# Query, key, gmlp-input and gate projections of a decoder layer as Strassen pairs kept in DRAM, with both attentions after them

## The chip, the cores and the metric

The kernel runs on one core of one Trainium2 chip. The metric is the device time of one execution in microseconds (us). A core has a matrix engine (TensorE, PE in the profile; its weight loads are the row PEld), a vector engine (VectorE, DVE), an activation engine (ScalarE, ACT), a general engine (GpSimd, POOL) and a queue from which the DMAs of this kernel are issued (SyncE, SP). On-chip tiles lie in SBUF, matmul results in eight PSUM banks, inputs, outputs and spilled tiles in DRAM.

## The reference

One layer (DEPTH is 1) for 1024 prompt positions and 64 sample positions (8 sequences of 8), model width 1024, all in float32:

```python
h = rmsnorm(x, norm_mix)
q, k, v, gu, gv, ga, gb = split_in(h @ w_in)      # 1024, 256, 256, 768, 768, 1024, 1024 columns
o = sink_attention(q, k, v, ...)                  # 16 heads of 64, 4 key heads, window 128, blocks of 128
vn = layernorm(gelu(gv), ln_g, ln_b)
s = gelu(gu) * (lower_triangular(ws) @ vn + bs)   # inside chunks of 128 positions, 6 groups of 128
merged = sigmoid(ga) * (o @ w_pa) + sigmoid(gb) * (s @ w_pb)
x = x + merged @ w_out
x = x + conv_ffn(rmsnorm(x, norm_ffn))            # up, causal conv of width 3, gelu gate, down
```

A final RMSNorm follows. Keys, values, convolution rows and normalised gmlp rows are outputs too.

## The kernel before

**Number format.** Every float32 operand of a matmul is split into a rounded high part and a remainder (`split`, L39 to L41: a ScalarE copy, then a VectorE subtraction), and a product is three matmuls: high by high, high weight by low operand, low weight by high operand. `mm3` (L215) does this for one tile of 128 output columns: 8 steps over the inner dimension, 3 matmuls each, over the token chunks of a group.

**Tokens.** They form two groups. Group 0 has 576 columns (64 sample, 512 prompt), in chunks of 320 and 256. Group 1 has 512 columns in one chunk.

**Weights.** The class `Weights` holds a list of weight tiles in the order of their use. It loads them by DMA into four raw buffers (`wraw`), splits them some units ahead (`emit`, tiles `wh`, `wl`), and `W.get()` hands out the next. In this order each weight of the first half stands twice, once per group.

**First half, per group** (the loop `for gr in groups`, L408 on): eight query tiles, two key tiles, the values (token-major, L551: activations are the stationary operand, 256 weight columns move), sixteen gate tiles, attention, gmlp inputs (`gu_tile`, and token-major gv), layer norm, the chunk mixing (`mix`, L863), then per output tile the two branch products with their gates (L901 to L907), then the output projection (`x1_tile`). Group 1 repeats this.

**Attention** (L709 on) runs in 16 steps per group, four key heads by four blocks. A step has three parts: `sc_p` (8 score matmuls, L727, then the softmax on ScalarE, VectorE and GpSimd), `tr_p` (4 transposes, L752, a split into `ph` and `pl`, and four GpSimd selections, L763), and `pv_p` (4 matmuls of 512 columns, L775, then a copy and additions, L777 and L782, and a split into `qo`). Parts of three steps overlap:

```python
for i in range(len(steps) + 2):
    if i >= 2:
        tr_p(*steps[i - 2])
    fill()
    if i < len(steps):
        sc_p(*steps[i])
    fill()
    if i >= 2:
        pv_p(*steps[i - 2])
```

`fill()` issues independent matmul work between the parts. Before, this is the gates: 32 half tiles of 4 inner steps (`gate_pieces`, L576), written to DRAM and read back for the merge. Group 0 has a sample attention of six iterations ahead of its steps (`sc_s`, L645, reads cached keys `ckt`).

**Second half.** The feed-forward block uses Strassen's scheme (7 products of half matrices in place of 8) for pairs of weight tiles: the class `Chain` (L1081) does the 7 products of one pair for one token group, 12 matmuls each (L1107) of 288 or 256 columns, in three PSUM banks. Its operands are 7 sums of activation halves per group, split (`tx`), and 7 sums of weight quarters (`total`, L165). The down projection (L1252) uses the scheme as well.

A scheduler in the build orders the instructions of each engine. On each engine, and on the SP queue, they then run in that order.

## Time and profile before

| what | value |
|---|---|
| median of 3 runs | 1609.77 us (1608.27 to 1610.48) |
| profiled execution | 1607.9 us, span 1605.9 us |
| PE / DVE / ACT / POOL busy in the span | 98% / 70% / 49% / 20% |
| DMA of the kernel | 215.07 MB, 40.1% of 16 DMA engines |
| first half, second half | 0 to 877 us, 877 to 1605.9 us |

"Busy" of an engine is the union of its instructions' durations. A matmul's duration holds its way through the array, so matmuls overlap, and the rate is read from how many start in a stretch. In the chain of waits a piece such as "PE mm L222 x762" is a run of matmuls that wait for nothing but each other.

### The profile page before, as it was taken

Reading aid. Unit: us, or ns where it says so; the run is one execution under the profiler, and the core shown is the slowest. Engines: PE = TensorE matmul, PEld = TensorE weight load, DVE = VectorE, ACT = ScalarE, POOL = GpSimd, SP = SyncE. Lnnn points to the kernel's source line nnn. Section 1 sums busy time; section 2 is a strip of 40 time slices with the busy share of each in tenths; the row PEclk is TensorE's granted clock in tenths of the full one; section 3 lists DMA queues with packets and bytes.
Section 4 is the critical chain, followed back from the end, with each engine's and each line's share of the span. In section 5 each row is a group of like instructions: output and inputs, shape, how many; then the busy total and the mean of one; then the engine's idle time right before and its main releaser. Section 6 shows DMA issues by size and latency. Waiting matters only on the chain.

```text
span 1605.9 us, 28256 instructions
## 1 busy us (share of the span) xinstructions
PE 1575.6 (98%) x11148; PEld 1490.7 (93%) x11148; DVE 1122.3 (70%) x1659; ACT 789.3 (49%) x1536; POOL 316.6 (20%) x432
## 2 busy tenths in 40 slices
PE   8999999999999999999999899999999999999997
PEld 8989999999998888898878899999999999999996
DVE  8546873654548777646457878898889778785676
ACT  7434664333345365544334555565565446353452
POOL 1302330100040343301002222222223222000023
PEclk9999999999999999999999999999999999999998
DMA  6322224134553622242565233332233225983453
GB/s 205 129 100 90 86 87 155 39 106 141 181 188 131 213 99 91 95 140 82 157 213 192 96 101 114 116 137 91 92 117 128 102 83 190 334 269 94 122 165 129
DMA packets 84147, 216.86 MB, mean 135 GB/s; under 512 B 9648, under 2 KB 15856, under 8 KB 84016
## 3 DMA queue, kind: packets, MB, share of 16 engines
q1 hardware_dynamic: 83872, 215.07, 40.1%
q8 instruction: 87, 1.43, 0.4%
q14 instruction: 44, 0.36, 0.1%
q10 hardware_dynamic: 144, 0.01, 0.0%
HBM read 168.82 MB, written 48.19 MB: 135 GB/s over the span
## 4 chain that ended last, share of the span: by engine, by line
PE 83%; DVE 7%; ACT 3%; POOL 2%; DMA 2%; issue 2%; SPq 0%; DVEq 0%; POOLq 0%; ACTq 0%
PE mm L222 32%; PE st L1107 28%; PE dn L1252 11%; PE mm L551 6%; DVE wl L41 2%; ACT s L742 1%; DMA wraw<-wt 1%; PE sc L727 1%; PE po L775 1%; POOL pl L763 1%; PE mm L863 1%; PE pt L752 1%; POOL ph L763 1%; DVE tl L41 1%; DVE nm L739 0%
## 5 line engine op out<-in xcount | busy, mean ns | idle before, releaser
L222 PE MATMUL mm<-hm,wh 128*128 128x320 f32 (+2 forms) x1920 | 429.7, 332 | 5.4 <-ACT hm L44 5.1
L1107 PE MATMUL st<-th,wl 128*128 128x288 f32 (+1 forms) x1232 | 356.3, 290 | 4.0 <-DVE wl L41 4.0
L1107 PE MATMUL st<-th,wh 128*128 128x288 f32 (+1 forms) x1232 | 357.6, 290 | 1.7 <-ACT wh L40 1.7
L1107 PE MATMUL st<-tl,wh 128*128 128x288 f32 (+1 forms) x1232 | 357.1, 290 | 0.0
L222 PEld LDWEIGHTS mm<-hm,wh 128*128 128x128 f32 x1920 | 302.0, 189 | 34.3 <-ACT hm L44 5.1
L40 ACT CAST wh<-wraw 128x512 fp32r<-128x512 f32 (+2 forms) x235 | 186.4, 801 | 236.7 <-PE mm L222 113.7
L222 PE MATMUL mm<-hm,wl 128*128 128x320 f32 (+1 forms) x960 | 264.4, 329 | 0.0
L41 DVE TENSOR_TENSOR wl<-wraw,wh 128x512 fp32r<-128x512 f32 (+2 forms) x235 | 220.5, 948 | 37.5 <-ACT wh L40 34.8
L1107 PEld LDWEIGHTS st<-th,wl 128*128 128x128 f32 x1232 | 234.4, 190 | 4.6 <-DVE wl L41 4.6
L1107 PEld LDWEIGHTS st<-th,wh 128*128 128x128 f32 x1232 | 234.9, 191 | 2.9 <-ACT wh L40 2.3
L1107 PEld LDWEIGHTS st<-tl,wh 128*128 128x128 f32 x1232 | 234.7, 191 | 0.0
L1252 PE MATMUL dn<-th,wh 128*128 128x288 f32 (+1 forms) x616 | 177.9, 289 | 2.5 <-DVE x L1262 2.5
L1252 PE MATMUL dn<-th,wl 128*128 128x288 f32 (+1 forms) x616 | 177.9, 289 | 0.0
L1252 PE MATMUL dn<-tl,wh 128*128 128x288 f32 (+1 forms) x616 | 177.7, 288 | 0.0
L222 PEld LDWEIGHTS mm<-hm,wl 128*128 128x128 f32 x960 | 159.1, 189 | 14.7
L1252 PEld LDWEIGHTS dn<-th,wh 128*128 128x128 f32 x616 | 116.4, 189 | 3.3 <-issue 2.6
L1252 PEld LDWEIGHTS dn<-th,wl 128*128 128x128 f32 x616 | 116.5, 189 | 0.1
L1252 PEld LDWEIGHTS dn<-tl,wh 128*128 128x128 f32 x616 | 116.5, 189 | 0.1
L551 PE MATMUL mm<-w2h,hm 128*128 128x256 f32 x576 | 104.2, 283 | 1.3 <-DVE vst L45 1.3
L40 ACT CAST wh<-ws 128x512 fp32r<-128x512 f32 x100 | 61.0, 621 | 63.9 <-PE st L1107 43.3
L551 PEld LDWEIGHTS mm<-w2h,hm 128*128 128x128 f32 x576 | 89.7, 191 | 1.6 <-DVE vst L45 1.5
L41 DVE TENSOR_TENSOR tl<-traw,th 128x544 fp32r<-128x544 f32 (+2 forms) x93 | 71.3, 774 | 22.6 <-ACT th L40 22.5
(239 smaller groups left out, 2631.3 us busy)
## 6 DMA issues: line engine op xcount, KB each, us to landing
wraw<-wt SPq DMA_DIRECT2D x171, 512.0 KB
traw<-td SPq DMA_DIRECT2D x77, 272.0 KB
td<-za SPq DMA_DIRECT2D x22, 544.0 KB
wraw<-wt SPq DMA_DIRECT2D x35, 256.0 KB
wraw<-wpb SPq DMA_DIRECT2D x16, 384.0 KB
td<-t SPq DMA_DIRECT2D x11, 544.0 KB
gate<-stg SPq DMA_DIRECT2D x16, 288.0 KB
stg<-gate SPq DMA_DIRECT2D x16, 288.0 KB
```

What stands on the lines that cost most here:

```text
L40: S.copy(hi, src)
L41: V.tensor_sub(lo, src, hi.bitcast(F32))
L222: PE.matmul(ps[:, lo:lo + c1 - c0], u[:, k, :], v[:, c0:c1], start=(k == 0 and i == 0), stop=(k == nk - 1 and i == 2))
L551: PE.matmul(ps, u[:, lo:lo + P], v[:, k, :], start=(k == 0 and i == 0), stop=(k == KD - 1 and i == 2))
L727: PE.matmul(ps[:, h, o0:256], q, kst[kv][:, e, k0:cur + P], start=e == 0, stop=e == 1)
L742: S.activation(s[:, h], s[:, h], AF.Exp, bias=nm[:, h:h + 1], accum_out=dn[:, h:h + 1])
L752: PE.transpose(pt[:, h * P:h * P + P], s[:, h, 0:P], ident)
L763: G.affine_select(t.rearrange("p (h q) -> p h q", h=4), src.bitcast(F32).rearrange("p (h q) -> p h q", h=4), [[0, 4], [-sign, P]], ALU.is_ ...
L775: PE.matmul(po, vst[b + d][:, kv, :], t, start=e == 0, stop=e == len(parts) - 1)
L863: PE.matmul(ps[:, mb + lo:mb + lo + P], v, wst[:, c, :], start=True, stop=True)
L1107: PE.matmul(ps, u[:, kk, :], v, start=first and kk + i == 0, stop=kk == 3 and i == 2, skip_group_check=True)
L1252: PE.matmul(place(m, e), u[:, m, :], v[:, lo:hi], start=new and i + k == 0 and (e == 0 or m % 2 == 0), stop=i == NU - 1 and k == 2, skip_g ...
```

## The change

All of the projection h @ w_in is now done for both groups ahead of attention.

1. Values and gv come first, token-major as before, group 0 then group 1. Beside them, group 1's h, the row norms, and the 7 sums of both groups are made (`t0_job`, `t1_job`). Group 1's sums go through DRAM.
2. Queries, keys, gmlp inputs and gates (32 tiles) become 16 Strassen pairs, done by the same `Chain` (moved up and given its places as an argument). The first two pairs run for group 0 alone, then 14 for both groups, then the first two for group 1. A pair's result is finished in `a_finish` (scaling and splitting of queries, splitting of keys, gelu, sigmoid) and written to DRAM.
3. Between products, layer norm and mixing of gv run as small jobs (`ln_job`, `mix_job`); the result s goes, split, to DRAM.
4. Attention of group 0 follows, then of group 1. Their operands are read from DRAM (`prepare`). `fill()` now issues the gmlp branch product of both groups (`branch`, parts of 2 inner steps) in the first, and the attention branch product of group 0 (`merge`) in the second.
5. Then the attention branch of group 1, and the output projection of both groups. The feed-forward sums of group 0 are made between tiles of the last one (`t0_first`) and no longer go through DRAM.

Each weight of a Strassen pair is loaded and split once (the first two pairs twice). The second half is as before.

```diff
-            for g in range(2):
-                for c in range(K0 + 2):
-                    W.add(wt(c), KD)
...
+            for (kind, c, d), _ in seq:
+                W.add_pair(wt(a_tiles[kind][0] + c), wt(a_tiles[kind][1] + d))
...
+            for at, (pair, gs) in enumerate(seq):
+                if at == FEWA + 6:
+                    qko.close()
+                if at == len(seq) - FEWA:
...
+                    prep = prepare(groups[0])
+                zs = {g: [zpa.tile([P, groups[g]["n"]], F32, name=f"z{e}{g}") for e in range(2)] for g in gs}
...
+                for j in range(7):
+                    w = W.get(3, 1)
+                    for ch in chains:
+                        ch.product(j, w)
+                    if jobs and 7 * at + j > 1:
+                        jobs.pop(0)()
+                    elif not jobs and lns and at > FEWA + 5 and j in (1, 3, 5):
+                        lns.pop(0)()
+                    elif prep:
+                        prep.pop(0)()
+                for g in gs:
+                    a_finish(pair, g, zs[g])
...
+            load_s(0, 0, NG)
+            for go in prep:
+                go()
+            load_s(1, 0, 4)
+            def branch(g, c):
...
+                        mm3(st["ps"], groups[g]["chunks"], st["w"], ss[g], k0, k0 + 2, NG)
+                        if k0 + 2 == NG:
+                            V.tensor_mul(st["t"], st["t"], st["ps"][:, base:base + n])
+                            nc.sync.dma_start(mbd[g][c], st["t"])
+            def merge(g, c, to):
...
+                        mm3(st["ps"], groups[g]["chunks"], st["w"], os_[g], k0, k0 + 2, KD)
+                        if k0 + 2 == KD:
+                            V.tensor_mul(st["t"], st["t"], st["ps"][:, base:base + n])
+                            V.tensor_add(st["t"], st["t"], st["u"])
+                            to(c, st["t"])
...
-                slots = {"n": len(pieces), "done": 0, "at": 0, "of": 36 + (12 if has_s else 0)}
+                slots = {"n": len(pieces), "done": 0, "at": 0, "of": 36 + (11 if has_s else 0)}
...
                         for i in range(6):
-                            fill()
+                            if i:
+                                fill()
                             if i >= 2:
                                 tr_s(i - 2)
                             if i < 4:
                                 sc_s(i)
...
+            pieces = [x for c in range(KD) for x in branch(0, c)] + [lambda: load_s(1, 4, NG)]
+            pieces += [x for c in range(KD) for x in branch(1, c)]
+            attention(groups[0], pieces)
...
+            for go in prepare(groups[1]):
+                go()
+            keep = lambda c, t: nc.sync.dma_start(msd[c], t)
+            for go in merge(0, 0, keep):
+                go()
+            attention(groups[1], [x for c in range(1, KD) for x in merge(0, c, keep)])
...
+            for c in range(KD):
+                if c == 1:
+                    rstd_first()
+                if 2 <= c < 6:
+                    t0_first(c - 2)
+                w, ps = W.get(1 if c < 7 else 4), acc2()
+                mm3(ps, groups[1]["chunks"], w, ms[1], 0, KD, KD)
+                x1_tile(groups[1], c, ps)
```

More of the change, by code (lines that the diff above doesn't have):

```diff
@@ new lines, in layer @@
+            xk = [hp0.tile([P, 576], F32, name=f"x{k}") for k in range(KD)]
+            places = [dest256(("v", 0), i)[1]() for i in range(2)]
+            W.start([p[2:] for p in places])
+            toks0 = groups[0]["toks"]
+            for x, parts in enumerate((((0, 0, 2), (1, 0, 2)), (), ((0, 2, 4), (1, 2, 4)),
+                                       ((0, 4, KD),), ((1, 4, KD),), (), (), ())):
+                for part in parts:
+                    W.load_part(*part)
+                dma = load_x(groups[0], x, xk[x])
@@ L1130, in conv, with up_chain @@
+        def up_chain(g, za, zb):
+            return Chain(g, tx, psu, up, lambda e, half: z_parts((za, zb)[e], g, half))
         def conv(i, z):
```

961 lines of the change are left out of this document (485 added, 476 removed).

## The prediction

> **What bounds the kernel now.** I read the page first: shares of the span, and the chain of waits.
>
> ```profile
> span 1605.9 us, 28256 instructions
> PE 1575.6 (98%) x11148; PEld 1490.7 (93%) x11148; DVE 1122.3 (70%) x1659; ACT 789.3 (49%) x1536; POOL 316.6 (20%) x432
> q1 hardware_dynamic: 83872, 215.07, 40.1%
> PE 83%; DVE 7%; ACT 3%; POOL 2%; DMA 2%; issue 2%; SPq 0%; DVEq 0%; POOLq 0%; ACTq 0%
> ```
>
> TensorE works nearly all the time, and the chain ends on it. So a change is worth the TensorE time it removes, less the idle time it opens. The same by stage (columns: stretch, its length, busy time of each engine with instruction counts, granted clock, DMA share, GB/s):
>
> ```profile
> 0.00:25.00 25.00, 19.75 (x125) 18.29 (x126) 18.84 (x30) 20.98 (x33) 0.20 (x4) 1.00 0.85 276
> 145.00:245.00 100.00, 99.00 (x715) 93.56 (x714) 77.06 (x136) 61.55 (x181) 37.53 (x64) 1.00 0.24 81
> 483.00:552.00 69.00, 67.73 (x339) 56.62 (x339) 54.34 (x65) 28.87 (x42) 15.29 (x15) 1.00 0.52 175
> 552.00:684.00 132.00, 130.62 (x646) 106.73 (x645) 96.25 (x162) 77.67 (x211) 49.48 (x78) 1.00 0.30 102
> 684.00:753.00 69.00, 68.44 (x456) 62.23 (x456) 38.77 (x54) 27.84 (x39) 5.91 (x1) 1.00 0.31 102
> 877.00:915.00 38.00, 32.27 (x228) 30.99 (x227) 30.84 (x56) 21.93 (x48) 9.92 (x14) 0.93 0.23 81
> 915.00:1349.00 434.00, 434.00 (x3439) 433.56 (x3438) 362.58 (x512) 235.28 (x467) 110.88 (x167) 1.00 0.32 111
> ```
>
> Both attentions (145 to 245, 552 to 684) are full today, with 1.0 and 1.4 us idle, because much gate work fills them. The Strassen stage (915 to 1349) is full too, with VectorE busy 84%. What TensorE work costs per instruction is read from pieces of the chain of waits (start, length, count):
>
> ```profile
> 251.70 43.20 PE mm L551 x360
> 335.73 100.58 PE mm L222 x762
> 842.95 33.99 PE mm L222 x144
> 912.47 436.73 PE st L1107 x3448
> ```
>
> That is 120.0 ns for 256 columns, 132.0 ns for a mean of 288 (chunks of 320 and 256), 236.0 ns for 512, and 126.7 ns for Strassen's mean of 272 (288 and 256). The slope is 116.0 / 256 = 0.453 ns a column, with only 4 ns fixed.
>
> **The matmuls removed.** Before, 32 tiles take 48 matmuls of 132.0 ns (group 0) and 24 of 236.0 ns (group 1): 12.0 us each, 384.0 us in all. After, 16 pairs take 84 + 84 matmuls of 126.7 ns: 21.28 us each, 340.5 us. **-43.5 us**, all of it on the path. Every other product keeps its instructions in the built program.
>
> Here the Trainium skill, page TensorE: Matmul & The Clock Gate, section Back-to-back issue gap, speaks against the change: it gives about 81 ns at 128 columns and 131 ns at 512 for sustained streams, so nearly a price per matmul. An estimate by a straight line between its two figures is 257 us before and 268 us after, 11 us more and a time of 1655 us; the 236.0 ns above contradicts its 131.
>
> **Attention.** The fill gets smaller. From the build: group 0's 16 steps have 13 parts of 12 matmuls at 132.0 ns and 24 of 6 at 236.0 ns, 54.6 us; group 1 has 28 of the first kind, 44.4 us. The step itself takes 8 x 120.0 + 4 x 236.0 ns and about 0.4 us of transposes, 2.3 us. So TensorE needs 91.4 us (5.7 a step) and 81.2 us (5.1 a step), where before a step took 100 / 15 = 6.7 us. What the others need is in the groups of VectorE between 145 and 245 us (busy, mean ns, idle before):
>
> ```profile
> L782 DVE TENSOR_TENSOR of<-po,ot 64x256 f32<-64x256 f32 x30 | 12.4, 413 | 1.8 <-ACT ot L777 1.4
> L745 DVE TENSOR_TENSOR s<-s,dn 128x512 f32<-128x512 f32 x15 | 11.3, 757 | 0.5
> L41 DVE TENSOR_TENSOR pl<-pt,ph 128x512 fp32r<-128x512 f32 x15 | 10.4, 692 | 0.5
> L41 DVE TENSOR_TENSOR wl<-wraw,wh 128x1024 fp32r<-128x1024 f32 x8 | 10.1, 1264 | 0.2
> L739 DVE TENSOR_REDUCE nm<-s 128x4 f32<-128x516 f32 x14 | 9.6, 684 | 0.9 <-POOL s L736 0.5
> L41 DVE TENSOR_TENSOR qo<-of,qo 128x256 fp32r<-128x256 f32 x15 | 8.4, 562 | 0.0
> L589 DVE TENSOR_TENSOR stg<-mm,nrs 128x576 f32<-128x576 f32 x11 | 8.3, 755 | 8.2 <-PE mm L222 8.0
> L733 DVE COPY_PREDICATED s<-c_mprev,sc 128x512 f32<-128x512 int32 x11 | 8.1, 740 | 0.3 <-ACT s L731 0.3
> L744 DVE RECIPROCAL dn<-dn 128x4 f32<-128x4 f32 x14 | 2.5, 177 | 10.7 <-ACT s L742 10.7
> ```
>
> ```profile
> L41 DVE TENSOR_TENSOR wl<-wraw,wh 128x768 fp32r<-128x768 f32 x16 | 15.3, 955 | 0.0
> L908 DVE TENSOR_TENSOR stg<-stg 128x576 f32<-128x576 f32 x8 | 6.0, 751 | 0.0
> ```
>
> One step costs VectorE 2 x 0.413 + 0.757 + 0.692 + 0.684 + 0.562 + 0.740 + 0.177 = 4.44 us. Group 0: 16 steps (four without the 0.740), 68.1 us, and 12.3 branch tiles of 0.955 + 0.72, together 88.7 us. Group 1: 71.0 us, and 7 tiles of 1.264 + 0.755 + 0.751, together 90.4 us. So VectorE needs 97% of TensorE's time in the first and 111% in the second, where it was at 77% and 73%. It also waits inside a step: 10.7 us in 14 steps for ScalarE's exponentials, unless other work stands there. The second attention is thus bound by VectorE and costs at least 9.2 us of TensorE idle. I allow 6 us in the first and 14 in the second (VectorE idle some 6% of the time). Ends: 9 for both with perfect interleaving, 41 if a step stays at 6.7 us. Less today's idle, 2.4 us and about as much again that overlapping matmuls cover: **+15 us**.
>
> **Entry into attention.** After the last pair, TensorE's next instruction is the sample score, which reads `ckt`. In the built program's SP queue that load stands behind the last two gate writes, and these wait for ScalarE's sigmoids of the last product. So nothing covers the load. Rows, from the chain, the tile `st`, ScalarE's groups, and two stretches around the idle time at 905 us:
>
> ```profile
> 88.58 4.09 DMA ckt<-ckt
> ```
>
> ```profile
> L1128 ACT ACTIVATE zb<-st x66: 198/347/394, 891.1 to 1357.1; 128x64 f32<-128x64 f32 x22, 128x224 f32<-128x224 f32 x22, 128x256 f32<-128x256 f32 x22
> ```
>
> ```profile
> L40 ACT CAST ph<-pt 128x512 fp32r<-128x512 f32 x15 | 8.8, 587 | 0.4
> ```
>
> ```profile
> 905.00:910.00 5.00, 1.60 (x11) 1.36 (x10) 4.38 (x10) 1.85 (x5) 1.27 (x2) 1.00 0.16 61
> 910.00:915.00 5.00, 3.38 (x12) 3.04 (x13) 4.83 (x10) 2.94 (x6) 0.17 (x1) 0.50 0.17 64
> ```
>
> The copy of 0.35 us, two sigmoids of about 0.59 us (priced as the 512-wide copy) and some 0.5 us of hand-overs make 2.0 us; the load 4.1 us. The first branch part then waits for its operand, which stands behind `ckt` and 0.26 MB of cached values: 0.85 MB, at 276 / 0.85 = 325 GB/s (the start, 0 to 25 us) 2.6 us, less 0.7 us of scores. Idle 8 us. After such idle time the clock falls to half (0.50 at 910 to 915), which costs up to 3 us more. **+11 us**, ends 6 (clock stays up, less to wait) and 17 (the 5.4 MB that the last two pairs put ahead are late; at 325 GB/s they need 16.6 of 20.2 us).
>
> **Smaller joints.** *Between the attentions*, loads of 1.7 MB (keys, queries) wait for the last `pv_p` and take 5 us at 325 GB/s; the merge parts placed there cover 3 of them by the built order: +2.5 us (0 to 6). *Sample attention*, with half the fill: +2 (0 to 5). *Start*: five token blocks before the norm is known, and more DMA in the first 40 us: +1.5 (0 to 4). *Operand sums*: making the T sums of group 0 between the last output tiles costs VectorE, per `t0_first`,
>
> ```profile
> 534.41 1.48 DVE hx L604
> ```
>
> 1.48 us of scaling, 0.9 of sums and 2.5 of splits (2016 elements at 1264 / 1024 ns), with 1.26 + 0.75 for the tile itself 6.9 us in 24 x 0.236 = 5.7 us of TensorE. Four times, that is 5 us late, of which two light tiles win half back. The stretch 877 to 915 shows that the next stage starts on VectorE anyway (32.27 of 38 us). +3.5 there, +2.5 for the same work at the head of the Strassen pairs: +6 (1 to 15). *Inside the pairs*, 7 splits, 4 sums and 4 additions leave VectorE under 93% even where three layer norms are added; beside the 84% that cost nothing I allow +1.5 (0 to 6). *Gone*: group 1's second start and gmlp joints, idle 1.3 and 0.6 us above, with hidden gaps **-5** (-2 to -6).
>
> **Sum.** -43.5 + 15 + 11 + 2.5 + 2 + 1.5 + 6 + 1.5 - 5 = **-9.0 us**. The profiled execution took 1607.9 us, 2.0 above its span; the median is 1.9 us above that, so all three shift alike: 1609.8 - 9.0 = **1600.8 us**. Less than 0.2% (3.2 us) can't be told from no change.
>
> **Rivals.** *The idle stays small.* If the schedule interleaves VectorE's work well (10 us in the attentions), the clock stays up at the entry (6 us) and the joints cost 6 us: -43.5 + 10 - 5 + 6 + 6 = -26.5, 1583 us. For it: the Strassen stage runs full at 84%. Against: nothing in the trace runs at 97%.
>
> *VectorE sets the pace of both attentions (slower).* If its order, tied to ScalarE's exponentials and GpSimd's selections, allows no step shorter than today's 6.7 us, fill was never what made a step long. TensorE idles 16 x 1.0 + 16 x 1.6 = 41 us in place of 20: +12, 1622 us. It decides from a mean step of 6.3 us (29 us idle), where the sum is zero. For it, a wait that exists today in steps with one fill part between `tr_p` and `pv_p`, though there is little to hide:
>
> ```profile
> 158.00 1.08 PE L775 MATMUL po<-pl,vst 128*128 128x512 f32 x2 [0.15 <-POOL pl L763]
> ```
>
> Against: VectorE idles 23% there, so 6.7 us need not be its floor.
>
> *DMA.* The built program moves 280 MB in place of 215, and 17 MB fall into the first 40 us of TensorE work after the pairs: 52 us at 325 GB/s. If loads needed at once stand behind others, some 10 us more: +1, 1611 us.
>
> *A price per matmul.* If a matmul's time did not fall with its columns, the 2688 matmuls of the pairs would cost today's mean of 384.0 / 2304 = 0.167 us each, 448 us in place of 384.0: +64 where the forecast has -43.5, 1708 us. The four chain rows exclude nearly all of this.
>
> **Chances.** Forecast 0.51 (its own range 1589 to 1607), small idle 0.17, VectorE's pace 0.23, DMA 0.08, price per matmul 0.01. Faster: 0.43 out of the forecast's 0.51, and all of the small idle's 0.17, 0.60. Same: 0.07 from the forecast, 0.02 from VectorE's pace, 0.04 from DMA, 0.13. Slower: the rest, 0.27. The range takes in the small idle's 1583 with a margin of 4 us and the VectorE rival with 4 us: 1579 to 1626.
>
> **What would show it.** Right: pairs at 126 to 127 ns a matmul and about 340 us; idle of 7 to 12 us ending on `ckt` with a halved clock after it; attention steps of 5.9 to 6.2 us with VectorE over 90% busy; idle at the feed-forward start above 6 us. Wrong: attention steps near 5.3 us (then 1583), above 6.3 (then slower), or TensorE idle inside the pairs.

## The result, and the profile after

The changed kernel takes 1615.1 us (median of 7 runs, 1612.5 to 1620.8); the ratio to the kernel before is 1.0039, 95% interval 1.0025 to 1.0054. It is slower by 0.4%, where 0.6% faster was forecast. The profiled execution took 1613.8 us with a span of 1612.0, 6.1 us more than before. Of all executions compared below, one alone ran in a slow state (1684.5 us at a mean granted clock of 0.843, where the others had 0.98 or more), and it is left out.

The page of the changed kernel:

```profile
span 1612.0 us, 30101 instructions
PE 1549.0 (96%) x11534; PEld 1487.0 (92%) x11534; DVE 1197.6 (74%) x1867; ACT 871.2 (54%) x1810; POOL 333.5 (21%) x458
PEclk9999999999997999999999899999999999999998
q1 hardware_dynamic: 127520, 280.16, 51.8%
PE 76%; DVE 9%; DMA 6%; ACT 3%; POOL 3%; issue 2%; SPq 1%; DVEq 0%; ACTq 0%; POOLq 0%
```

TensorE is busy 27 us less than before (1575.6), in a span 6 us longer; its share of the chain of waits fell from 83% to 76%, and transfers rose from 2% to 6%. So TensorE work did go, and waiting came. The stages, in the windows view (stretch, length, busy time of TensorE, its weight loads, VectorE, ScalarE and GpSimd, granted clock, DMA share, GB/s):

```profile
118.30:140.00 21.70, 17.14 (x109) 16.85 (x107) 12.74 (x24) 10.40 (x22) 4.92 (x5) 0.84 0.81 262
140.00:340.00 200.00, 199.89 (x1599) 199.21 (x1598) 146.43 (x254) 137.85 (x266) 17.57 (x19) 1.00 0.54 182
340.00:360.00 20.00, 16.94 (x121) 16.55 (x121) 12.22 (x19) 9.71 (x23) 2.38 (x3) 0.91 0.69 245
479.40:500.00 20.60, 11.24 (x64) 8.38 (x63) 6.42 (x14) 7.12 (x16) 0.72 (x1) 0.60 0.98 364
531.00:647.00 116.00, 112.08 (x686) 95.31 (x685) 94.21 (x170) 73.34 (x219) 41.49 (x71) 1.00 0.62 200
660.00:741.20 81.20, 73.71 (x449) 60.99 (x447) 70.22 (x122) 49.87 (x155) 43.25 (x62) 1.00 0.46 149
835.00:884.00 49.00, 43.49 (x192) 34.53 (x192) 45.80 (x52) 22.19 (x33) 21.44 (x14) 1.00 0.50 162
884.00:922.40 38.40, 32.84 (x208) 31.90 (x208) 31.56 (x56) 21.10 (x47) 11.13 (x15) 0.87 0.23 80
```

In order: the head of the Strassen pairs, the pairs at full speed, the first gmlp mixing jobs among them, the entry into attention, the two prompt attentions, the end of the output projection, and the start of the feed-forward. Only the second stretch is full. "Idle" below is the length of a stretch less what its matmuls cost at full clock, shape by shape (median from start to start), so it holds the half clock too. By that count the added idle time is about 50 us, against 34.5 in the forecast: 43.5 us of matmuls went, and the span still grew by 6.1.

Pieces of the chain of waits (start, length, what):

```profile
129.23 178.72 PE st L274 x1404
...
345.67 6.54 DMA vn<-vnd
...
473.39 8.54 DMA sg1d<-z
...
483.88 4.17 DMA ckt<-ckt
```

The pairs run at 178.72 / 1404 = 127.3 ns a matmul, as forecast. The three transfers are the ends of waits that come up again below.

### The profile page after: what moved, and what is told of

Its sections match the earlier page's. It is cut to its first block, busy times and chain, and to the rows that moved or that the text cites. A ratio compares the mean times of both kernels' runs of the same rounds, so it can differ in the third digit from the quotient of the medians.

```text
span 1612.0 us, 30101 instructions
## 1 busy us (share of the span) xinstructions
PE 1549.0 (96%) x11534; PEld 1487.0 (92%) x11534; DVE 1197.6 (74%) x1867; ACT 871.2 (54%) x1810; POOL 333.5 (21%) x458
## 4 chain that ended last, share of the span: by engine, by line
PE 76%; DVE 9%; DMA 6%; ACT 3%; POOL 3%; issue 2%; SPq 1%; DVEq 0%; ACTq 0%; POOLq 0%
PE st L274 44%; PE mm L220 11%; PE dn L1346 10%; PE st L468 7%; DVE wl L41 2%; DMA wraw<-wt 2%; POOL pl L996 2%; DVE tl L41 1%; PE po L1008 1%; ACT s L975 1%; POOL ph L996 1%; PE sc L958 1%; PE mx L664 1%; PE pt L985 1%; DMA sg1d<-z 1%
## 5 line engine op out<-in xcount | busy, mean ns | idle before, releaser
L274 PE MATMUL st<-th,wh 128*128 128x256 f32 (+1 forms) x2128 | 619.4, 291 | 13.4 <-ACT ku L255 4.6
L274 PE MATMUL st<-tl,wh 128*128 128x256 f32 (+1 forms) x2128 | 616.4, 290 | 0.9 <-DVE tl L41 0.9
L274 PE MATMUL st<-th,wl 128*128 128x256 f32 (+1 forms) x2128 | 615.3, 289 | 0.5 <-DVE wl L41 0.5
L274 PEld LDWEIGHTS st<-th,wh 128*128 128x128 f32 x2128 | 405.8, 191 | 16.6 <-ACT ku L255 4.8
L274 PEld LDWEIGHTS st<-th,wl 128*128 128x128 f32 x2128 | 405.4, 191 | 0.9 <-DVE wl L41 0.9
L274 PEld LDWEIGHTS st<-tl,wh 128*128 128x128 f32 x2128 | 405.2, 190 | 1.1 <-DVE tl L41 1.1
L41 DVE TENSOR_TENSOR wl<-ws,wh 128x512 fp32r<-128x512 f32 x172 | 120.7, 711 | 40.2 <-ACT wh L40 39.2
L468 PE MATMUL st<-w2h,hh 128*128 128x256 f32 x288 | 83.2, 289 | 6.4 <-ACT hh L44 6.4
L468 PE MATMUL st<-w2h,hl 128*128 128x256 f32 x288 | 82.8, 287 | 0.0
L468 PE MATMUL st<-w2l,hh 128*128 128x256 f32 x288 | 82.7, 287 | 0.0
```

Source lines behind the costliest of these rows:

```text
L41: V.tensor_sub(lo, src, hi.bitcast(F32))
L274: PE.matmul(ps, u[:, kk, :], v, start=first and kk + i == 0, stop=kk == 3 and i == 2, skip_group_check=True)
L468: PE.matmul(ps, u[:, lo:lo + P], v[:, k, :], start=k + i == 0, stop=k == KD - 1 and i == 2)
```

## The experiments

Times are compared through the ratio to the kernel before, which ran on the same chip each time: a difference of 0.001 is 1.6 us, and each ratio is known to between 0.001 and 0.002. "Against the changed kernel" is the difference to 1.0039, which has its own uncertainty, so that a gain of less than about 3 us can't be told from none. Stage lengths are read from the start of the first and last product of a stage.

**Is a product worth its own time?** One more product per pair, read by nobody:

```diff
                     for ch in chains:
                         ch.product(j, w)
+                        if j == 6:
+                            ch.again(w)      # 12 matmuls into a bank of its own
```

> The changed kernel with an eighth product in each Strassen pair, into a bank of its own that nothing reads: 32 x 12 matmuls more, 48.9 us by the trace's 0.133 and 0.120 us for 288 and 256 columns and by no other work. Theory that the pairs are bound by TensorE, so that a product fewer or more is worth its own time: 1664 us (+47 to +50). Rival (the pairs are paced by the splits of weights or by transfers, so that the seven products of a pair are not worth their time): +35 us or less, 1650 us or less.

Measured: 1648.3 us, ratio 1.0242 [1.0224, 1.0260], 32.7 us against the changed kernel: the rival's number, yet not its reason. In the profiled execution (span 37.9 us longer, the slowest of the four) the time from the first product of the pairs to the first sample score grows from 370.2 to 408.4 us, 38 us for 48.9 us of matmuls, and the rest is idle time that disappears: 5 us at the mixing job, and the gap ahead of the sample score, 9.0 us before, is 3.1. Between them the pairs stay full (199 of 200 us). So TensorE sets the pace inside the pairs, but some 11 us of idle exist only because the pairs are short, and both gaps end on a transfer in the chain above. That a product taken out returns less than its price in the same way is argued from this, not shown.

**The entry into attention.** Three edits: (a) mask, first cached keys and values loaded during the last pairs; (b) the keys, queries and values of the prompt attention moved out from there into the sample attention, and two branch operands (`sx`) put in their place; (c) staging tiles of their own for the last pair's gates.

```diff
                 def samples():
...
+                    nc.sync.dma_start(gr["ckt"], a["ckt"][0])      # (a)
+                    nc.sync.dma_start(gr["msamp"], a["msamp"])
+                    nc.sync.dma_start(gr["cv"], a["cv"][0])
...
-                return ([samples] if g == 0 else []) + [operands(0)] + [value(x) for x in names] + [operands(1)]
+                gr["later"] = [operands(0)] + [value(x) for x in names] + [operands(1)]   # (b)
+                return [samples, lambda: load_first(2)] if g == 0 else gr["later"]
...
-                zs = {... zpa.tile(...) ...}
+                zs = {... zpa.tile(...) if at < len(seq) - 1 else stage(512) ...}         # (c)
...
                         for i in range(6):      # sample attention
...
+                            gr["later"][i]()                                              # (b)
```

All three:

> The changed kernel with another order of transfers at the end of the pairs: the sample mask, the first cached keys and values and the operands of two branch tiles are loaded during the last two pairs, in front of the last gate writes; keys, queries and values of the prompt attention, which were there, are loaded during the sample attention; the last pair's gates go to staging tiles of their own, so that they don't wait for the write of the pair before. Nothing is computed differently. Theory of the queue (the 13.4 us of idle time at the entry come from what SP's queue puts in front of the cached keys, and from the half clock after it): idle 479 to 497 falls to about 5 us, no half clock longer than 7 us, time about 8 us less, 1607 us. Rival of the bytes (the same 10 MB have to land around the entry whatever their order): idle stays above 10 us, time 1612 us or more.

Measured: 1603.2 us, ratio 0.9965 [0.9952, 0.9977], 11.9 us against the changed kernel, and faster than the kernel before. Its windows at the entry:

```profile
480.00:485.00 5.00, 5.00 (x54) 3.98 (x52) 2.81 (x5) 4.07 (x7) 0.91 (x1) 1.00 0.99 317
485.00:490.00 5.00, 4.58 (x36) 3.78 (x36) 2.55 (x8) 2.33 (x9) 0.00 (x0) 1.00 1.00 378
```

TensorE stays busy and the clock at 1.00, while the transfers run at 0.99 to 1.00 as before: the bytes were not the trouble, their order was. Part (a) alone, which aims at the wait that the changed kernel has here (releaser, us in total, times, longest):

```profile
PE sc L876 <- DMA ckt<-ckt: 8.7, 1, 8.7
```

> The changed kernel with only the sample mask and the first cached keys and values loaded during the last two pairs; keys, queries and values of the prompt attention stay there, behind them, and the operands of the branch tiles are loaded where they were. Tells apart the three parts of the edit at the entry that gained 11.9 us. Theory that the cached keys' place in the queue is most of it, as forecast: 6 us or more, 1609 us or less. Rival (the first product of the branch tiles, whose operands come behind 2.3 MB of prompt queries and the last gate writes, waits in place of the score): scores start at once, then TensorE stands at the branch tile; 0 to 4 us, 1611 to 1615 us.

Measured: 1613.3 us, ratio 1.0037 [1.0025, 1.0050]: 0.3 us, nothing that can be told from none. The score no longer waits for `ckt`; what TensorE waits for between 478 and 532 us is now:

```profile
PE sc L884 <- ACT s L892: 6.5, 1, 6.5
PE pt L911 <- ACT s L899: 3.5, 1, 3.5
```

The second score waits 6.5 us for ScalarE to copy the first one out of its bank. The rival was right that something else waits, though it named the branch tile. In the chain shown above, the last gate's negated product waits for the write of the pair before (`sg1d<-z`, 8.54 us, slow behind 4 MB of prompt operands), ScalarE's sigmoid for that, and in ScalarE's order the copy stands behind the sigmoid. So without (c):

> The edit at the entry without its last part: the last pair's gates go to the same tiles as before, so that their computation waits for the write of the pair before (8.5 us in the trace of the changed kernel). Theory (with the 4 MB for the prompt attention out of the way this write is short, and nothing urgent stands behind the last gates): as the whole edit, 1603 to 1605 us. Rival (that wait is what holds SP's queue, and the operands of the branch tiles behind it): 4 us or more are lost of the 11.9, 1607 us or more.

Measured: 1606.1 us, ratio 0.9981 [0.9971, 0.9991], 9.3 us of the 11.9, a little short of the theory's 1603 to 1605. In its trace the last gates no longer wait for the write of the pair before (their negated product follows the last matmul by 0.8 us). So (b) is what pays, (c) adds 2.6 us (inside the uncertainty of two ratios), and (a) is worth nothing alone; whether (b) pays without (a) was not run.

**The attentions.** The product with the values comes one step later, behind the next step's transposes and a fill part:

```diff
-                                    t = ap.tile([P, 512], F32R, name=f"p{nm}{d}")
+                                    t = ap.tile([P, 512], F32R, name=f"p{nm}{d}", bufs=2)
...
-                    for i in range(len(steps) + 2):
-                        if i >= 2:
+                    for i in range(len(steps) + 3):
+                        if 2 <= i < len(steps) + 2:
                             tr_p(*steps[i - 2])
                         fill()
+                        if i >= 3:
+                            pv_p(*steps[i - 3])
                         if i < len(steps):
                             sc_p(*steps[i])
                         fill()
-                        if i >= 2:
-                            pv_p(*steps[i - 2])
```

> The changed kernel with both prompt attentions pipelined one step deeper: the product with the values follows its transposes one step later, behind the next step's transposes and a part of the fill, and the four selected tiles have two buffers. Instructions are the same. Theory of the chain (a step waits from its transposes over ScalarE's copy, VectorE's subtraction and four selections on GpSimd to the product with the values, about 5 us with the hand-overs, for which one to two fill parts and the scores are too short a cover): idle of TensorE in both attentions falls from 25 us to under 10, time about 1600 us. Rival of VectorE's pace (the step is as long as VectorE's work on it): idle falls by no more than 4 us, time 1611 to 1615 us, VectorE at over 90% of the stretch.

Measured: 1605.9 us, ratio 0.9983 [0.9972, 0.9994], 9.0 us against the changed kernel. From first to last transposes, the changed kernel:

```profile
541.00:624.00 83.00, 79.08 (x443) 64.08 (x443) 74.37 (x133) 60.62 (x186) 37.46 (x60) 1.00 0.54 177
648.00:735.00 87.00, 80.79 (x510) 68.94 (x509) 77.08 (x135) 57.61 (x182) 49.16 (x73) 1.00 0.52 165
```

and the deeper pipeline:

```profile
543.50:625.00 81.50, 76.85 (x450) 65.39 (x448) 72.16 (x133) 61.29 (x186) 36.74 (x60) 1.00 0.56 180
648.70:726.00 77.30, 73.24 (x492) 66.09 (x492) 73.17 (x131) 57.17 (x178) 45.43 (x73) 1.00 0.53 175
```

The second attention falls from 87.0 to 77.3 us, 15 steps of 5.80 and 5.15 us; the first hardly moves. Neither forecast came: by the prices of the matmuls the idle time of the two falls by some 9 us, from 23.2 to 14.6; the rival allowed 4 us, the theory wanted 15. What TensorE waits for in these stretches, in the second attention of the changed kernel and of the deeper pipeline:

```profile
PE po L1008 <- POOL pl L996: 5.5, 9, 0.8
```

```profile
PE po L1008 <- POOL pl L996: 0.3, 1, 0.3
```

and in the first of the two kernels:

```profile
PE pt L985 <- DVE s L978: 1.1, 2, 0.9
```

```profile
PE pt L985 <- DVE s L978: 4.4, 4, 1.7
```

So in the second it was above all the chain within a step, which ends on GpSimd, that held TensorE, not VectorE's sum; with the chain covered VectorE is at 73.17 / 77.30 = 95%. In the first, TensorE waits more for VectorE's `s` instead. What made the chain long is seen in the timeline of the changed kernel (start, us, engine, line):

```profile
695.24 1.22 POOL L996 TENSOR_SCALAR_AFFINE_SELECT pl<-pl 128x512 fp32r<-128x512 f32 x2 [0.29 <-DVE pl L41]
...
700.66 2.66 POOL L996 TENSOR_SCALAR_AFFINE_SELECT pl<-pl 128x512 fp32r<-128x512 f32 x2 [0.31 <-DVE pl L41]
...
701.17 1.65 DVE L41 TENSOR_TENSOR wl<-wraw,wh 128x1024 fp32r<-128x1024 f32 x1
```

Two selections take 1.22 us, and 2.66 us where a weight split of VectorE falls on them, which itself takes 1.65 us where such splits took 1.26 us before. The Trainium skill, page SBUF — State Buffer, section Who interferes with whom, says that a VectorE instruction with two inputs in SBUF contends with a GpSimd instruction that reads SBUF, over a read port that the two share. The rows agree as far as a slowdown of both goes. Whether VectorE is the next limit, on the kernel with the deeper pipeline:

```diff
-                        split(oh[kv][:, :, c0:c0 + P], ol[kv][:, :, c0:c0 + P], of)
+                        S.copy(oh[kv][:, :, c0:c0 + P], of)
+                        G.tensor_sub(ol[kv][:, :, c0:c0 + P], of, oh[kv][:, :, c0:c0 + P].bitcast(F32))
```

> The kernel with the attentions pipelined one step deeper, and the remainder of each step's output (0.42 to 0.56 us on VectorE, 16 times in each attention) subtracted on GpSimd. With the deeper pipeline the second attention took 77.3 us in place of 86.9 between its first and last transposes, with VectorE busy 73.2 of them (95%). Theory that VectorE is what limits it now: the second attention gets shorter by 4 to 7 us, the first by 1 to 3, time 1598 to 1601 us. Rival (GpSimd, at 59% there, or the port that both share gets in the way: GpSimd's selections took 1.02 us in the second attention, 0.64 where VectorE was quiet): no gain or a loss of up to 4 us, 1606 to 1610 us.

Measured: 1607.7 us, ratio 0.9990 [0.9979, 1.0000]; no gain over 0.9983. The second attention:

```profile
645.00:724.20 79.20, 74.21 (x499) 66.25 (x499) 71.50 (x119) 58.16 (x183) 59.28 (x87) 1.00 0.57 181
```

VectorE has 12 instructions fewer and is busy only 1.7 us less: part of what is moved to GpSimd (8.0 us) comes back as longer instructions, such as the product of `s` and `dn`, 0.99 us in place of 0.82. The rival holds; that VectorE alone is the next limit isn't shown.

**The head of the pairs.** The waits of the changed kernel between 115 and 150 us, of TensorE, ScalarE and VectorE:

```profile
PE st L274 <- ACT ku L255: 4.6, 1, 4.6
...
ACT th L40 <- DMA stg<-t1d: 9.2, 6, 5.6
...
DVE x L560 <- DMA x<-xt: 5.8, 2, 5.4
```

First the 16 jobs that load and split group 1's operand sums were started later in the program:

```diff
-                    if jobs and 7 * at + j > 1:
+                    if jobs and 7 * at + j > 4:
                         jobs.pop(0)()
+                        if jobs and 7 * at + j > 8:
+                            jobs.pop(0)()
```

> The changed kernel with the 16 jobs that load and split the operand sums of group 1 at the head of the pairs started three products later and then two to a product, as many as before. Theory of the head (the 7.7 us of idle time at 118 to 140 us come from ScalarE waiting in order for these loads, which delays the copies that free TensorE's banks, and from the half clock after it): idle there falls to about 2.5 us, 1610 us. Rival (the work of the splits itself is too much there, whenever it comes): the idle time moves into the second pair and stays at 6 us or more, 1614 us.

Measured: 1615.8 us, ratio 1.0039 [1.0027, 1.0052], nothing. The scheduler put the first casts back in the same place on ScalarE, which waits 5.6 us for the load as before, so this tests nothing. Then with the order held:

```diff
+                    with tc.issue_after(Chain.mark["keep"].ins):
                         split(*(t[:, lo:hi] for t in txa[1][kk]), x)
```

> As the first try at the head of the pairs, and now the order on ScalarE is held too: the scheduler may put the casts of group 1's loaded operand sums only behind the last kept product that was traced before them (in the first try it put them in front all the same, and the stretch 118 to 140 us ran as before, with 7.6 us of excess in place of 7.6). Theory of the head (ScalarE waits 5.6 us in order for a load, and the copies that free TensorE's banks stand behind it; half clock follows): idle of 118 to 140 us falls from 7.7 to about 2.5 us, time about 1610 us. Rival (these splits are too much work there, whenever they come): idle moves into the second and third pair, time 1614 us or more.

Measured: 1619.4 us, ratio 1.0061 [1.0043, 1.0078], rather slower. The same waits in this run:

```profile
PE st L276 <- ACT kn L259: 6.8, 2, 5.7
...
ACT wh L40 <- DVE ws L163: 8.4, 1, 8.4
...
DVE x L562 <- DMA x<-xt: 5.9, 3, 5.2
```

Read upward: VectorE stands 5.2 us in order at the load for the last of group 1's operand sums (as it did in the changed kernel), the sums of weights stand behind it, ScalarE's casts behind these. So the sums were made sooner:

```diff
-            jobs = [none] + [x for kk in range(4) for x in (t0_job(kk), none)] + [t1_job(kk) for kk in range(4)]
+            jobs = [none] + [x for kk in range(4) for x in (t0_job(kk), t1_job(kk))]
```

> The changed kernel with the operand sums of group 1 made between those of group 0, so that their loads and their writes are done some 10 us sooner. The second try at the head of the pairs (casts held back on ScalarE) only moved the wait: VectorE stood 5.2 us at the load of the last of these sums, with the sums of weights queued behind it. Theory of the queue (the load stands on SP behind writes that wait, and VectorE and ScalarE stand in order behind it): idle of 118 to 140 us falls from 7.7 to under 3 us, time about 1610 us. Rival of the transfers (the DMA engines are busy 0.9 to 1.0 from 116 to 128 us, so whatever is late stays late): idle 6 us or more, there or up to 20 us sooner, 1614 us or more.

Measured: 1616.0 us, ratio 1.0052 [1.0039, 1.0065], no gain. In the combined kernel below, which has the same edit, the idle time of 120 to 140 us is 9.5 us against 7.6, so this moves the wait once more. Last, the loads were left out, and with them the sums:

```diff
-            jobs = [none] + [x for kk in range(4) for x in (t0_job(kk), none)] + [t1_job(kk) for kk in range(4)]
+            jobs = [none] + [x for kk in range(4) for x in (t0_job(kk), none)]
...
-                    x = stage(512).rearrange("p (h c) -> p h c", h=2)[:, :hi - lo]
-                    nc.sync.dma_start(x, t1d[kk][:, lo:hi])
+                    x = rsg[1].rearrange("p (h c) -> p h c", h=2)[:, :hi - lo]
```

> The changed kernel without the operand sums of group 1: their loads, VectorE's and GpSimd's work on them, their writes and the loads back are left out, and the 16 splits at the head of the pairs read a resident tile in place of them (so group 1's products of the pairs are made from other values; TensorE's work is the same). Two edits that only move this work left the time as it was. Theory of the head (the stretch 118 to 140 us loses 7.7 us, half clock included, to these transfers and what queues behind them): idle there under 2 us, time 1608 to 1610 us. Rival (time won here is lost again at the entry into attention, which waits for transfers that don't come sooner): end of the pairs 6 us sooner, but first sample score at the same time as before, 1613 us or more.

Measured: 1610.2 us, ratio 1.0003 [0.9993, 1.0012], 5.8 us against the changed kernel. Its windows:

```profile
124.00:128.00 4.00, 4.00 (x32) 4.00 (x32) 3.90 (x8) 4.00 (x9) 0.00 (x0) 1.00 0.02 4
128.00:132.00 4.00, 4.00 (x32) 4.00 (x31) 4.00 (x8) 3.98 (x8) 2.21 (x1) 1.00 0.01 4
```

VectorE and ScalarE are full with the same splits and TensorE never waits; the last product of the pairs comes 6.4 us sooner and the gap after it stays (10.1 us, 9.0 before). So the head costs some 6 us of its own, and they come from making the sums and moving them through memory, not from the splits. Which of the two, the run doesn't tell, since it leaves out both; the waits above end on loads of both kinds (`x`, for making them, and `t1d`, for reading them back).

**The first mixing job.** TensorE waits 3.1 us at 349 us for `vn`, and runs at half clock after it. Its loads one job ahead:

```diff
+                mix_load(0, 0)             # at the end of mix_first
...
+                    if (g, c) != (1, NG - 1):
+                        mix_load(*((g, c + 1) if c + 1 < NG else (1, 0)))
+                    vn, gu = mixed.pop((g, c))
```

> The changed kernel with the loads of each gmlp mixing job (normed inputs, gelu inputs) issued one job ahead. Theory of the load (TensorE stands 3.2 us at 349 us for the first such load, and runs at half clock after it, 5.6 us in all between 340 and 460): idle there falls to about 1 us, time 1610.5 us. Rival (the load waits for the layer norm's result in memory, whenever it is issued): idle stays at 4 us or more, time 1614 to 1615 us.

Measured: 1617.0 us, ratio 1.0050 [1.0035, 1.0066], no gain: the scheduler left the first load and its product 4 us apart (wait 3.6 us, load 7.7 us). Then two empty places behind the load, with the order held on TensorE:

```diff
-            lns += [mix_first] + [mix_job(g, c) ...]
+            lns += [mix_first, none, none] + [mix_job(g, c) ...]
...
+                        with tc.issue_after(Chain.mark["mm"].ins):
                             PE.matmul(ps[:, 0:NS], vn[0:NS, 0], late["wss"][:, c, :], start=True, stop=True)
```

> The changed kernel with the first gmlp mixing job two places later than the load of its operands, and TensorE's first product of each job held behind the last Strassen product traced before it (in the first try the load still came only 4 us ahead of its product, and TensorE stood 3.6 us). Theory of the load (6.5 to 7.7 us from issue to landing, so a product that comes 4 us after the issue waits): idle of 340 to 460 us falls from 5.6 to about 1 us, time 1610 us. Rival (what doesn't wait here waits at the entry into attention, where the transfers are late anyway): idle there grows by as much, 1614 to 1616 us.

Measured: 1613.1 us, ratio 1.0039 [1.0027, 1.0051]. The wait is gone and the time is not:

```profile
340.00:360.00 20.00, 19.66 (x158) 19.46 (x157) 13.31 (x24) 12.10 (x25) 2.40 (x3) 1.00 0.64 221
479.70:500.00 20.30, 10.19 (x60) 7.32 (x59) 5.71 (x11) 6.98 (x16) 0.73 (x1) 0.62 0.98 370
```

In the first stretch 2.7 us more of TensorE work are done at full clock, in the entry 1 us less than in the changed kernel (11.24 of 20.60), and the pairs begin 2.3 us later in this execution. The rival is supported and not proved.

**The join to the feed-forward.** The reciprocal of group 0's norm by way of 128x5 values:

```diff
-                V.reciprocal(nacc0, nacc0)                       # 128x576
+                V.reciprocal(rt[:, 0:5], rt[:, 0:5])             # one column per token block
...
+                    S.activation(dg[:, lo:lo + w_], ident[:, o:o + w_], AF.Copy, scale=rt[:, i:i + 1])
+                    PE.matmul(rs[:, lo:lo + w_], ones, dg[:, lo:lo + w_], start=True, stop=True)
+                S.copy(nacc0, rs[:, 0:576])
```

> The changed kernel with the norm between output projection and feed-forward computed otherwise: the reciprocals of group 0 are taken on 128x5 values of one matmul per token block and spread again by a product of ones with a diagonal, in place of one reciprocal over 128x576 (3.75 us on VectorE at 837 us). Theory of VectorE (at 835 to 884 us it is busy 45.8 of 49 us, TensorE idles 6.8 us there and 11.5 us in the feed-forward start behind it, so 3.5 us less work at its head comes back in full): idle of 835 to 922 falls from 18.3 to about 14 us, time 1611 us. Rival (the stretch is set by the four operand sums and the feed-forward start by its own operands, whatever precedes them): 0 to -1 us, 1614 us; the added hand-overs between TensorE and ScalarE could also cost 1 to 2 us.

Measured: 1617.2 us, ratio 1.0047 [1.0030, 1.0065], no gain. TensorE now waits 2.3 us for ScalarE's diagonals in the norm itself, and VectorE 3.7 us for the spread result: the hand-overs take what the shorter reciprocal gives. Then VectorE was relieved of the remainders:

```diff
-                split(th[:, 1:5], tl[:, 1:5], t4)      # and so for the other two parts
+                    S.copy(th[:, j], src if len(src.shape) == 3 else src[:, None])
+                    S.copy(tl[:, j], src if len(src.shape) == 3 else src[:, None])
```

> The changed kernel with the remainders of group 0's feed-forward operands copied on ScalarE in place of subtracted on VectorE (so they hold other values): 12 instructions, 12.8 us of VectorE's 45.8 in the stretch 835 to 884 us by the trace, go to ScalarE, which is busy 22.2 of 49 there. Theory of VectorE (each of the four operand sums takes VectorE 6.5 us beside 1.8 us for the tile itself, where TensorE needs 5.7, so it falls behind): idle from 835 to the end of the feed-forward start falls from 18.3 to about 9, what the start had before the change, time 1606 us. Rival (the order of hand-overs between VectorE, GpSimd and ScalarE in one sum sets it): 14 us or more of idle, 1611 us or more.

Measured: 1610.4 us, ratio 1.0009 [0.9999, 1.0018], 4.8 us against the changed kernel. 87.4 us from the same place on, first in the changed kernel, then in this one:

```profile
835.00:922.40 87.40, 76.33 (x400) 66.43 (x400) 77.37 (x107) 43.29 (x79) 32.57 (x28) 0.94 0.38 126
```

```profile
838.20:925.60 87.40, 78.92 (x446) 69.01 (x446) 73.81 (x106) 53.33 (x97) 30.19 (x29) 0.98 0.41 135
```

TensorE does 46 matmuls more and the clock is 0.98 in place of 0.94. Neither forecast came in full: relieving VectorE gives back 4.8 us, about half of the 9.6 us that the join loses; what the rest hangs on isn't shown.

**Together.** Entry and deeper pipeline:

> The changed kernel with the two edits that gained: the other order of transfers at the entry into attention, and the attentions pipelined one step deeper. Theory that the two losses are separate: both gains add up, 11.9 and 9 us less than 1615, 1594 us. Rival (the deeper pipeline only hides the same late transfers): 1600 us or more.

Measured: 1596.2 us, ratio 0.9924 [0.9907, 0.9941]: 18.5 us against the changed kernel, where 11.9 and 9.0 sum to 20.9. The two losses are separate within the uncertainty, and this version beats both kernels. With the earlier sums and the later mixing jobs as well:

> As the kernel with both gaining edits, with the earlier operand sums of group 1 and the later mixing jobs as well. Theory that all four losses are separate: 1584 to 1586 us. Rival (time gained ahead of the pairs' end is given back at the entry, which is set by transfers): 1591 us or more.

Measured: 1598.3 us, ratio 0.9943 [0.9930, 0.9955], no better. With the later mixing jobs alone:

> The kernel with both gaining edits, and the later first mixing job. Alone the later mixing job took the idle time of 340 to 360 us away and didn't move the time. Theory that the entry into attention, late by its transfers, took it back, and that the new order of transfers there no longer does: 1591 us, 5 less than without. Rival (the mixing job's gain is lost elsewhere or is within the spread of the half clock's periods): 1595 us or more.

Measured: 1597.5 us, ratio 0.9924 [0.9910, 0.9937], no better. The profiled executions, each the fastest of its six, show where some of the 5 us may go. First the one with the mixing edit, then the one without, some 30 us behind the end of the pairs:

```profile
507.00:517.00 10.00, 9.99 (x62) 7.95 (x61) 3.81 (x10) 3.27 (x12) 0.00 (x0) 0.59 0.24 89
```

```profile
508.00:518.00 10.00, 9.30 (x82) 7.79 (x79) 6.30 (x19) 4.86 (x14) 0.00 (x0) 1.00 0.71 196
```

TensorE is full in the first and does 62 matmuls in place of 82, at half clock for most of the stretch, after a gap of under 2 us in the sample attention. One execution of each is no proof. In the kernel with all the edits the clock stays at 1.00 there, and it is no faster either: its half clock at the join lasts 20.5 us, in two periods, where the kernel without the mixing edit and the earlier sums has 10.2.

## Why the prediction was wrong

The direction failed on the idle time, about 50 us in place of 34.5; the matmuls came out as reckoned. The steps that failed are the term of the operand sums, 6 us, which measured 17.3, and the load inside the pairs that was taken for covered, 1.5 us, which measured 5.6. The two largest terms, entry and attentions, came out 2.4 and 2.5 us above the forecast, and in good part by another mechanism than it gave.

*Matmuls removed, -43.5.* Right in size: 127.3 ns a matmul against 126.7, the pairs full, which also ends the rival of a price per matmul. What the step didn't see is that a shorter stage gives its transfers less time: with an eighth product in each pair 11 us of idle vanish.

*Entry, +11 forecast, 13.4 measured* from 479 to 497 us (gap 9.0 us, ending on `ckt`, half clock until 500.6). The forecast had the place, the wait and the clock right and the reason wrong. It priced the load's place behind the gate writes, and the run that moves only that gains 0.3 us. What pays is the order of the 4 MB for the prompt attention, moved together with that load: 9.3 us of 11.9. The forecast had put the case that these bytes are late only at the end of its range.

*Attentions, +15 and +2.5 for their join; measured +20.* Idle is 10.0 and 15.3 us at matmul prices, and 0.9 at the join, against some 6 today. VectorE's need stood near the forecast: 94.2 us beside 106.0 of TensorE's own time in the first (89%, 97% forecast), 70.2 beside 65.9 in the second (107%, 111% forecast). What failed is the step from need to limit: busy 81% and 86% of the stretches, VectorE was not the one that ended the waits. In the second its need accounts for 70.2 - 65.9 = 4.3 of the 15.3 us; of the other 11.0, the deeper pipeline takes away 9.7. The row that the text quoted for the rival of VectorE's pace, TensorE waiting for `pl`, was the mechanism there: the chain over GpSimd inside one step (5.5 us of waits in the second attention, 0.3 with the deeper pipeline). What makes the 10.0 us of the first stays open. That rival itself, which needed steps over 6.3 us, fell: they took 5.5 and 5.8, even under the 5.9 to 6.2 of the forecast (and, read the same way, 6.4 and 7.3 before, where the forecast had 6.7 for both). Less of the fill lay inside them: by the prices of its matmuls 2.9 and 2.6 us a step, where the forecast had 3.4 and 2.8.

*Operand sums, +6 forecast, 17.3 measured: 7.7 at the head, where 2.5 stood, and 9.6 at the join, where 3.5 stood.* The largest miss. At the join three rows of VectorE in 835 to 884 us show it:

```profile
L1112 DVE SCALAR_TENSOR_TENSOR x<-x,c_gains,rs 128x576 f32<-128x576 f32 x8 | 8.4, 1068 | 0.0
L41 DVE TENSOR_TENSOR tl<-x,th 128x288 fp32r<-128x288 f32 (+1 forms) x8 | 7.4, 928 | 0.0
L1103 DVE RECIPROCAL rs<-rs 128x576 f32<-128x576 f32 x1 | 3.8, 3753 | 1.4 <-ACT rs L1102 1.4
```

Scaling takes 8 x 1.07 us in place of 4 x 1.48, the remainders 7.4 us, and 5.4 more on `t`, in place of 4 x 2.5, and the reciprocal of 3.75 us was in no term of the sum. That these are the loss is shown in part: without the remainders 4.8 us come back, without the long reciprocal none. At the head the forecast priced VectorE's work; there VectorE and ScalarE stand at loads, and without the sums and their transfers 5.8 us come back.

*Inside the pairs, +1.5; measured 5.6* at the first mixing job, whose load takes 6.5 us and was taken for covered. *Start, +1.5; measured +2.6. Sample attention, +2; measured +1.2. Gone, -5:* near that. These terms add up to some 55 us; where the difference to 50 lies isn't shown.

*The clock.* The forecast counted half clock at the entry alone, 3 us. These are the periods of the changed kernel:

```profile
128.50:135.30 6.80, 6.07 (x25) 6.07 (x26) 6.20 (x13) 3.39 (x9) 1.88 (x2) 0.50 0.79 251
353.80:357.20 3.40, 3.40 (x17) 3.40 (x17) 2.14 (x3) 0.58 (x2) 0.04 (x1) 0.50 0.28 82
483.50:500.60 17.10, 11.65 (x65) 8.98 (x66) 5.67 (x12) 5.65 (x13) 0.00 (x0) 0.50 1.00 368
886.30:893.10 6.80, 6.80 (x32) 6.80 (x31) 2.42 (x5) 2.53 (x8) 0.00 (x0) 0.50 0.19 68
917.00:920.40 3.40, 3.40 (x15) 3.40 (x16) 3.40 (x8) 2.52 (x5) 0.17 (x1) 0.50 0.25 94
```

31.3 us of TensorE work were done at half speed, which costs about half of that, 15.7 us; before, two such periods, at 910 and 1558 us, held 8.6 us of work, 4.3 us. So about 11 of the some 50 us are the clock's, behind five waits of 2 to 9 us.

The DMA rival (transfers late behind others, 10 us more, 1611 us) had a chance of 0.08 and comes nearest to what the entry, the head and the mixing job showed. The measured 1615.1 us lies inside the stated range because the range took in the rivals; that isn't to the credit of the sum.

## What to carry to other kernels

Where a change takes work from the engine that is full, price also what the work was covering: here the transfers around the shortened stage kept their length, and uncovered waits of 2 us and more were paid again in clock. A wait that ends on one load isn't priced by that load; look through the queue for what comes next, since here removing the named wait gained nothing, and doing so together with a new order of the bytes behind it gained 12 us. Where an attention's fill shrinks, one step more of lag between transposes and the product with the values is worth trying: here it cost only buffers and gained 9.0 us.

## What the runs showed of the hardware

The starts of the five periods of half clock lie on one grid: 353.8 - 128.5, 483.5 - 353.8, 886.3 - 483.5 and 917.0 - 886.3 us are 66, 38, 118 and 9 times 3.413 us, each within 0.1 us, and their lengths are 1, 2 and 5 such windows. The window ahead of the one that starts at 353.8 held 1.9 us of idle time (to 352.2 us), and so did the one ahead of 886.3 (to 884.8): the clock fell after work had resumed. A gap of 1.3 us at 739 us brought none. The other traces bear this out. In each of 18 all changes of the clock lie on one grid of 3.413 us, to 0.01 us, and on these grids, the first and last 20 us left out, all 71 windows at full clock that held 1.8 us of idle time or more were followed by half clock, 7 of 27 with 1.46 to 1.8 us, and 3 of 308 with 0.5 to 1.45 us. Four windows with less than 0.5 us were followed by it too, all in the sample attention, whose matmuls are small; why is open. The Trainium skill, page TensorE: Matmul & The Clock Gate, Part 1, describes a free-running window of 3413 ns, and these runs agree; by its table the clock falls after an idle window, while here one that was half idle was enough.

Since the grid lies differently against each execution, it could also make a spread, which is argued here and not shown: in 7 runs the changed kernel's span goes from 1610.8 us at a mean granted clock of 0.987 to 1619.0 at 0.981, while the kernel before stays within 2.2 us beside it (in the 17 runs beside the kernel with the shorter reciprocal, within 8.2).

In the one place shown, an affine selection of 128x512 on GpSimd goes from 0.61 to 1.33 us beside a subtraction of two operands in SBUF on VectorE, and that subtraction from 1.26 to 1.65 us. A reciprocal of 128x576 values on VectorE took 3.75 us, five times an addition of that size (0.75).
